# A decoder step with product-key experts: the gate table written by scattering DMAs instead of one-hot products, the sample tokens' experts gathered in the trunk

## The chip, the cores and the metric

One core of a Trainium2 chip runs the whole program in one launch. The metric is the device time of an execution in microseconds. The core has TensorE (PE, matmuls; PEld are its weight loads), VectorE (DVE), ScalarE (ACT), GpSimd (POOL, which also issues indirect DMAs) and SyncE (SP, which issues the plain DMAs).

## The reference, cut to what matters

1024 prompt tokens and 64 sample tokens (8 sequences of 8) go through one decoder layer with the same weights, in float32, width 1024:

```
xn = rmsnorm(x);  lru_x, lru_gate, q, k, v, ga, gb = split(xn @ w_in)
A = rglru(conv(lru_x)) * gelu(lru_gate);  B = window_attention(q, k, v)
hres = x + (sigmoid(ga) * (A @ w_branch_lru) + sigmoid(gb) * (B @ w_branch_attn)) @ w_out
xt = rmsnorm(hres);  qr = xt @ w_query                  # 8 heads x 2 x 128
s_top, i_top = top_k(qr . sub_keys, 16)                 # of 128, per head and half
best, pos = top_k(s_top[0] + s_top[1], 16)              # of 256 sums, per head
idx = i_top[0] * 128 + i_top[1] at pos;  g = softmax(best)   # 128 experts of 16384 per token
y = hres + sum_e gelu(xt . U[idx_e]) * g_e * V[idx_e]
```

So each token needs 128 rows of U and 128 rows of V, of 1024 numbers each.

## The kernel before, in words

**Precision.** A float32 matrix is split into a part hi, rounded to the matmul's format, and lo = x - hi. `split` does hi on ACT (line 148) and lo on VectorE or GpSimd (line 149); `mm3` multiplies hi x hi, hi x lo and lo x hi (lines 168 to 170), three matmuls for each tile of weights.

**Trunk.** `trunk` runs three times, over blocks of 256 prompt tokens with the 64 sample tokens (320 columns), 384 and 384 prompt tokens. Each block goes through attention, the gates with `w_branch_attn`, the recurrent branch (`lru`), the merge with `w_branch_lru`, `w_out`, the second norm, and `retrieve` (the product with `w_query`, the sub-keys and the sixteen best of each half). Weights come through SP's queue in pieces of 512 KB (`load_c`, `load_n`), three raw buffers and three split ones, 84 pieces for each block; GpSimd computes their lo parts.

**Which experts.** `choose` takes a block's tokens in tiles of 128 rows and finds for each head the sixteen best of 50 candidate sums and, by comparing positions (`eq`, VectorE, with a product on GpSimd), the experts' numbers.

**Two ways to apply experts.** The last block's 384 tokens (NA) are *gathered*: for each of 3 tiles and 128 slots GpSimd issues an indirect DMA that fetches one row of U (later of V) for each of the 128 tokens, and VectorE multiplies and sums it (lines 847 and 859). The other 704 tokens (ND, sample tokens among them) are *dense*: `dense` multiplies them with all 16384 rows of U and V, 128 experts e at a time, in two halves of 352 columns, and weights the activations with a table `g_d` of gates, which is zero where a token doesn't use an expert. Gathers run beside the dense loop: after each e some are issued (`pump`), so that all are done after 120 (PACE) of the 128.

**The gate table before.** For every 4 dense tokens `build_g` makes one-hot matrices of the upper and lower half of the experts' numbers (lines 889 and 890), multiplies the first with the gates in three bf16 parts (891 on GpSimd, 892, 893) and lets 12 matmuls add them into a 128x128 table per token (896 to 898); ACT copies it out (899), and SP writes 2 MB for 32 tokens (901). `slots_T` has transposed indices and gates before that.

**Order.** The functions `choose` and `build_g` of one block are generators. The next block's trunk takes a number of their steps (`bg`, numbers in PG1 and PG2) after chosen instructions, and all that is left at its end. The framework's planner then orders instructions on each engine by priority and simulated time, and each engine runs its list in order. The last block's `choose` runs at the start of the dense stage, before the gathers.

Of the kernel before, what the change touches and what calls it, by code (L numbers as in the profile page):

```python
# [8 lines left out]
F32 = mybir.dt.float32  # L9
# [10 lines left out]
P = 128  # L20
# [34 lines left out]
PAUSE = 17  # L55
# [7 lines left out]
CH = 32  # L63
# [6 lines left out]
class Kern:  # L70
    def __init__(self, ctx, tc, i, o):
# [8 lines left out]
        self.g_d = self.dr.tile([ND // CH, P, P, CH], F32, name="g_d")  # L80
        self.kcar_d = self.dr.tile([P, NKV, P], F32, name="kcar_d")
        self.sT_d = self.dr.tile([P, 3, ND], F32, name="sT_d")
        self.xn2h_d = self.dr.tile([P, KD, ND], F32, name="xn2h_d")
        self.xn2l_d = self.dr.tile([P, KD, ND], F32, name="xn2l_d")
        self.xn2n_d = self.dr.tile([NA, D], F32, name="xn2n_d")

    def setup(self, c):
# [5 lines left out]
        nc.vector.tensor_copy(self.iota, iota[:, 0:NCAND])  # L93
        self.iota4 = c.tile([P, P, 4], BF16, name="iota4")
        nc.vector.tensor_copy(self.iota4, iota.unsqueeze(2).to_broadcast([P, P, 4]))
# [90 lines left out]
    def load_c(self, src, c0):  # L186

        nc, sp = self.nc, self.sp
        hi = sp.tile([P, KD, P], F32R, tag="whi", name="whi", bufs=NW)
        lo = sp.tile([P, KD, P], F32R, tag="wlo", name="wlo", bufs=NW)  # L190
        raw = sp.tile([P, KD, P], F32, tag="wraw", name="wraw", bufs=NR)
        nc.sync.dma_start(raw, src.rearrange("(k p) c -> p k c", p=P)[:, :, c0:c0 + P])
        self.split(hi, lo, raw, nc.gpsimd)
        return hi, lo

    def load_n(self, src, c0):
# [3 lines left out]
        for h in range(2):  # L200
# [4 lines left out]
            self.split(hi, lo, raw, nc.gpsimd)  # L205
# [61 lines left out]
    def trunk(self, bi, x, raw, bg):  # L267
# [5 lines left out]
        self.pg = PG2 if bi == len(BLOCKS) - 1 else PG1  # L273
# [4 lines left out]
        self.attention(bi, xh, xl, ah, al, raw, bg)  # L278

# [17 lines left out]
        self.otag = "s4"  # L297
        self.lru(bi, n, nP, xh, xl, lh, ll, bg)
        self.otag = "sb"
# [36 lines left out]
        for t, (c0, r) in enumerate(tiles):  # L336
            keep = self.xn2n_d[r0 + c0 - ND:r0 + c0 - ND + r, :] if r0 >= ND else None
            self.norm_T(hr[0:r, t, :], r, gb, yh, yl, c0, keep)
            bg(self.pg[4])
        if r0 < ND:  # L340
            nc.sync.dma_start(self.xn2h_d[:, :, r0:r0 + n], f32(yh))
            nc.sync.dma_start(self.xn2l_d[:, :, r0:r0 + n], f32(yl))
# [24 lines left out]
    def attention(self, bi, xh, xl, ah, al, raw, bg):  # L367
# [46 lines left out]
        def scores(t, j, qT):  # L414
# [28 lines left out]
            nc.gpsimd.tensor_tensor(sb[:, :, 0:S], sb[:, :, 0:S], z4.unsqueeze(2).to_broadcast([P, 4, S]), op=ALU.mult)  # L443
# [299 lines left out]
    def choose(self, bi):  # L743
# [5 lines left out]
        late = []  # L749
        for t, (c0, r) in enumerate(tiles):  # L750
# [21 lines left out]
            for h in range(PH):  # L772
# [7 lines left out]
                yield  # L780
            bf = xp.tile([P, PH, TOPK], F32, tag="bf", name="bf", bufs=1)
            nc.vector.tensor_copy(bf[0:r], bi_[0:r])
            ev = xp.tile([P, PH, TOPK], F32, tag="ev", name="ev", bufs=1)
            for h in range(PH):
                eq = xp.tile([P, TOPK, NCAND], F32, tag="eq", name="eq", bufs=2)
                nc.vector.tensor_tensor(eq[0:r], self.iota[0:r].unsqueeze(1).to_broadcast([r, TOPK, NCAND]),
                                        bf[0:r, h].unsqueeze(2).to_broadcast([r, TOPK, NCAND]), op=ALU.is_equal)
                nc.gpsimd.tensor_tensor(eq[0:r], eq[0:r], ce[0:r, h].unsqueeze(1).to_broadcast([r, TOPK, NCAND]), op=ALU.mult)
                nc.vector.tensor_reduce(ev[0:r, h], eq[0:r], axis=AX.X, op=ALU.add)
                yield  # L790

            if r0 >= ND:
                gv = self.gA[:, t]
            else:
                ft = xp.tile([P, 3, NSLOT], F32, tag="ft", name="ft", bufs=2)
                gv = ft[:, 2].rearrange("p (h s) -> p h s", h=PH)
# [6 lines left out]
            nc.vector.tensor_tensor(gv[0:r], bv[0:r], sz[0:r].unsqueeze(2).to_broadcast([r, PH, TOPK]), op=ALU.mult)  # L803
            if r0 >= ND:
                nc.vector.tensor_copy(self.iA[:, t], ev)
            else:
                e32 = xp.tile([P, NSLOT], I32, tag="bi", name="e32", bufs=1)
                i12 = xp.tile([P, 2, NSLOT], I32, tag="cd", name="i12", bufs=1)
                nc.vector.tensor_copy(e32[0:r], ev[0:r].rearrange("p h s -> p (h s)"))
                nc.vector.tensor_scalar(i12[0:r, 0], e32[0:r], 7, None, op0=ALU.arith_shift_right)  # L810
                nc.vector.tensor_scalar(i12[0:r, 1], e32[0:r], 127, None, op0=ALU.bitwise_and)
                nc.vector.tensor_copy(ft[0:r, 0:2], i12[0:r])
                late.append((ft, r, r0 + c0))
                if len(late) > 1:
                    self.slots_T(*late.pop(0))
                yield
        for u in late:
            for _ in range(PAUSE):
                yield
            self.slots_T(*u)  # L820

    def slots_T(self, ft, r, n0):

        nc = self.nc
        pt = self.tr((P, 3, P))
        for x in range(3):
            nc.tensor.transpose(pt[:, x, 0:r], ft[0:r, x], self.ident[0:r, 0:r])
        sl = self.xp.tile([P, 3, P], F32, tag="sl", name="sl", bufs=1)
        nc.scalar.copy(sl[:, :, 0:r], pt[:, :, 0:r])
        nc.sync.dma_start(self.sT_d[:, :, n0:n0 + r], sl[:, :, 0:r])  # L830


    def gather_steps(self, gp, gps):
        nc, i, o = self.nc, self.i, self.o
        for t in range(NA // P):
# [16 lines left out]
            nc.sync.dma_start(st, self.hres_d[ND + t * P:ND + (t + 1) * P, :])  # L852
# [10 lines left out]
            nc.sync.dma_start(o["y"][ND + t * P:ND + (t + 1) * P, :], st)  # L863
# [6 lines left out]
    def build_g(self, bi):  # L870

        nc, sp = self.nc, self.sp
        p0, p1, smp, nP, n, tiles = self.geom(bi)
        for ch in range(ROW0[bi] // CH, (ROW0[bi] + n) // CH):
            sg = sp.tile([P, AT], F32, tag="at", name="sg", bufs=1)[:, 0:P * CH].rearrange("p (i n) -> p i n", i=P)
            sT = sp.tile([P, 3, CH], F32, tag="sT", name="sT", bufs=1)
            nc.sync.dma_start(sT, self.sT_d[:, :, ch * CH:(ch + 1) * CH])

            s16 = sp.tile([P, 5, CH], BF16, tag="s16", name="s16", bufs=1)
            nc.scalar.copy(s16[:, 0:3], sT)  # L880
            for x in (2, 3):
                nc.vector.tensor_tensor(sT[:, 2], sT[:, 2], s16[:, x], op=ALU.subtract)
                nc.vector.tensor_copy(s16[:, x + 1], sT[:, 2])
            for t4 in range(CH // 4):
                n0 = t4 * 4
                col = lambda x: s16[:, x, n0:n0 + 4].unsqueeze(1).to_broadcast([P, P, 4])
                oij = self.sp.tile([P, 4, P, 4], BF16, tag=self.otag, name="oij", bufs=N4 if self.otag == "s4" else 6)
                oj, wh, wm, wl = (oij[:, x] for x in range(4))
                nc.vector.tensor_tensor(oj, self.iota4, col(1), op=ALU.is_equal)
                nc.vector.tensor_tensor(wh, self.iota4, col(0), op=ALU.is_equal)  # L890
                nc.gpsimd.tensor_tensor(wl, wh, col(4), op=ALU.mult)  # L891
                nc.vector.tensor_tensor(wm, wh, col(3), op=ALU.mult)
# [208 lines left out]
```

## Time and profile before

| | us |
|---|---|
| median of 3 runs (lowest, highest) | 4002.96 (3999.92, 4014.38) |
| the profiled execution | 3999.96 |
| its span, first to last instruction | 3998.0 |
| PE, DVE, ACT, POOL busy | 3641.4 (91%), 3151.0 (79%), 1290.8 (32%), 2407.2 (60%) |
| DMA | 821.75 MB, 206 GB/s over the span |

Busy times are shares of the span over stages with different limits. Matmuls are pipelined, and the trace models their ends, so that the busy times of neighbouring ones overlap; how fast a stream of them runs is seen from start to start. The granted clock is a share of TensorE's full speed. An idle time is put down to the instruction that ended it.

### The profile page before, as it was taken

Reading aid. Unit: us, or ns where it says so; the run is one execution under the profiler, and the core shown is the slowest. Engines: PE = TensorE matmul, PEld = TensorE weight load, DVE = VectorE, ACT = ScalarE, POOL = GpSimd, SP = SyncE. Lnnn points to the kernel's source line nnn. Section 1 sums busy time; section 2 is a strip of 40 time slices with the busy share of each in tenths; the row PEclk is TensorE's granted clock in tenths of the full one; section 3 lists DMA queues with packets and bytes.
Section 4 is the critical chain, followed back from the end, with each engine's and each line's share of the span. In section 5 each row is a group of like instructions: output and inputs, shape, how many; then the busy total and the mean of one; then the engine's idle time right before and its main releaser. Section 6 shows DMA issues by size and latency. Waiting matters only on the chain. (4 is left out here: it accounts for less than half of the span.)

```text
span 3998.0 us, 60600 instructions
## 1 busy us (share of the span) xinstructions
PE 3641.4 (91%) x22734; PEld 3477.6 (87%) x22734; DVE 3151.0 (79%) x6798; ACT 1290.8 (32%) x2346; POOL 2407.2 (60%) x1560
## 2 busy tenths in 40 slices
PE   7988998778897878998899999999999999999998
PEld 6778978668895777888799999999999999999998
DVE  6365787999899988998987777777777777777773
ACT  4454353443333435333222222222222222222221
POOL 3444546565554664764576677767766767676651
PEclk8989999889997988999899999999999999999999
DMA  5334523234441133444359898999989899899972
GB/s 148 100 111 149 154 72 90 79 101 145 171 139 56 58 94 108 138 173 162 125 204 308 292 318 303 321 323 316 322 295 311 306 319 316 309 317 310 319 259 80
DMA packets 505654, 821.75 MB, mean 206 GB/s; under 512 B 34220, under 2 KB 360812, under 8 KB 502000
## 3 DMA queue, kind: packets, MB, share of 16 engines
q1 hardware_dynamic: 394768, 415.18, 32.5%
q0 software_dynamic: 110592, 402.70, 28.2%
q8 instruction: 178, 2.92, 0.3%
q14 instruction: 116, 0.95, 0.1%
HBM read 753.25 MB, written 66.50 MB: 205 GB/s over the span
## 5 line engine op out<-in xcount | busy, mean ns | idle before, releaser
L149 POOL TENSOR_TENSOR wlo<-wraw,whi 128x1024 fp32r<-128x1024 f32 x252 | 639.3, 2544 | 513.7 <-ACT whi L148 476.0
L168 PE MATMUL ou<-ah,vh 128*128 128x352 f32 x2048 | 663.4, 327 | 40.6 <-ACT ah L148 23.3
L168 PE MATMUL sc<-dx,uh 128*128 128x352 f32 x2048 | 664.6, 325 | 16.2 <-ACT uh L148 9.0
L169 PE MATMUL ou<-al,vh 128*128 128x352 f32 x2048 | 660.1, 325 | 5.3 <-DVE al L149 5.0
L170 PE MATMUL sc<-dx,ul 128*128 128x352 f32 x2048 | 662.0, 323 | 1.0 <-POOL ul L149 1.0
L169 PE MATMUL sc<-dx,uh 128*128 128x352 f32 x2048 | 662.5, 324 | 0.0
L170 PE MATMUL ou<-ah,vl 128*128 128x352 f32 x2048 | 659.0, 324 | 0.0
L859 DVE SCALAR_TENSOR_TENSOR acc<-row,hv,acc 128x1024 f32<-128x1024 f32 x384 | 493.1, 1284 | 157.3 <-DMA row<-in_expert_v,iA 151.6
L847 DVE SCALAR_TENSOR_TENSOR row<-row,xt 128x1024 f32<-128x1024 f32 x384 | 465.5, 1217 | 174.3 <-DMA row<-in_expert_u,iA 165.0
L857 POOL DMA_INDIRECT row<-in_expert_v,iA x384 | 362.2, 943 | 267.8 <-DVE acc L859 192.6
L845 POOL DMA_INDIRECT row<-in_expert_u,iA x384 | 362.4, 944 | 264.4 <-DVE row L847 187.4
L168 PEld LDWEIGHTS ou<-ah,vh 128*128 128x128 f32 x2048 | 385.0, 189 | 55.7 <-ACT ah L148 29.7
L168 PEld LDWEIGHTS sc<-dx,uh 128*128 128x128 f32 x2048 | 386.9, 189 | 20.0 <-DVE al L149 9.8
L148 ACT CAST whi<-wraw 128x1024 fp32r<-128x1024 f32 x252 | 263.9, 1049 | 429.6 <-PE mm L169 167.6
L169 PEld LDWEIGHTS ou<-al,vh 128*128 128x128 f32 x2048 | 387.0, 189 | 7.8 <-DVE al L149 7.8
L170 PEld LDWEIGHTS sc<-dx,ul 128*128 128x128 f32 x2048 | 386.5, 189 | 1.4 <-POOL ul L149 1.4
L169 PEld LDWEIGHTS sc<-dx,uh 128*128 128x128 f32 x2048 | 387.2, 189 | 0.0
L170 PEld LDWEIGHTS ou<-ah,vl 128*128 128x128 f32 x2048 | 386.8, 189 | 0.0
L970 DVE TENSOR_TENSOR dac<-dac,ou 128x352 f32<-128x352 f32 x672 | 339.3, 514 | 59.9 <-PE ou L170 58.0
L149 POOL TENSOR_TENSOR vl<-vn,vh 128x1024 fp32r<-128x1024 f32 x128 | 309.0, 2422 | 65.6 <-ACT vh L148 38.5
L149 POOL TENSOR_TENSOR ul<-un,uh 128x1024 fp32r<-128x1024 f32 x128 | 310.7, 2427 | 45.7 <-ACT uh L148 43.6
L891 POOL TENSOR_TENSOR oij<-oij,s 128x512 bf16<-128x512 bf16 x176 | 225.1, 1290 | 176.9 <-DVE oij L890 132.7
(287 smaller groups left out, 8484.5 us busy)
## 6 DMA issues: line engine op xcount, KB each, us to landing
wraw<-in_w_in SPq DMA_DIRECT2D x132, 512.0 KB
un<-in_expert_uT SPq DMA_DIRECT2D x128, 512.0 KB
vn<-in_expert_v SPq DMA_DIRECT2D x128, 512.0 KB
g_d<-sg SPq DMA_DIRECT2D x22, 2048.0 KB
gt<-g_d SPq DMA_DIRECT2D x64, 704.0 KB
wraw<-in_peer_w_query SPq DMA_DIRECT2D x48, 512.0 KB
wraw<-in_w_branch_attn SPq DMA_DIRECT2D x24, 512.0 KB
wraw<-in_w_branch_lru SPq DMA_DIRECT2D x24, 512.0 KB
```

What stands on the lines that cost most here:

```text
L148: nc.scalar.copy(hi, src)
L149: return (lo_eng or nc.vector).tensor_tensor(lo, src, f32(hi), op=ALU.subtract)
L168: nc.tensor.matmul(ps, lh, rh, start=first and j == 0, stop=False)
L169: nc.tensor.matmul(ps, lh, rl, start=False, stop=False)
L170: nc.tensor.matmul(ps, ll, rh, start=False, stop=last and j == n - 1)
L845: nc.gpsimd.indirect_dma_start(out=row, out_offset=None, in_=i["expert_u"], in_offset=bass.IndirectOffsetOnAxis(ap=ia[:, s:s + 1], axis=0))
L847: nc.vector.scalar_tensor_tensor(row, row, 1.0, xt, op0=ALU.mult, op1=ALU.mult, accum_out=hv[:, s:s + 1])
L857: nc.gpsimd.indirect_dma_start(out=row, out_offset=None, in_=i["expert_v"], in_offset=bass.IndirectOffsetOnAxis(ap=ia[:, s:s + 1], axis=0))
L859: nc.vector.scalar_tensor_tensor(acc, row, hv[:, s:s + 1], acc, op0=ALU.mult, op1=ALU.add)
L891: nc.gpsimd.tensor_tensor(wl, wh, col(4), op=ALU.mult)
L970: nc.vector.tensor_tensor(ac[k // 4][:, k % 4, a:b], ac[k // 4][:, k % 4, a:b], ps[:, 0:b - a], op=ALU.add)
```

## The change

The dense stage takes 640 tokens, all prompt tokens of the first two blocks, in two parts of 256 and 384 columns (before: 704, in 352 and 352). The gate table is ten tables of 64 tokens. `zero_g` zeroes them in the first block with 40 DMAs of 1 MB from a zero tile. `choose` computes for each slot the position expert x 64 + token in its table, and `chain` issues 64 indirect DMAs for each table, which add one weight each for 128 (token, slot) pairs: 640 scatters in all. Scatters into the same table follow one another; those of different tables take turns. `slots_T` and `build_g` go.

The 64 sample tokens' experts are gathered in the trunk, two slots in one DMA (64 tokens on each half of the partitions): 64 rows of U in the second block (`early_u`), 64 of V in the third (`early_v`). `behind` mixes a step of `choose`, one of the early gathers and three (second block) or four (third) scatters into each background step.

The lo parts of all trunk weights, and the scaling of the attention's probabilities, go from GpSimd to VectorE. The expert's number is found by subtracting positions and taking the smallest absolute value, without GpSimd.

```diff
-ND = NTOT - NA
+ND = NTOT - NA - NS
+COL0 = [0, BLOCKS[0][1]]
+RA = ROW0[-1]
+NT2 = 64
+STEP = 32768
+SCAT = (3, 4)
-PAUSE = 17
+PG0 = (1, 1, 1, 0, 0, 0, 0, 0)
...
-        self.g_d = self.dr.tile([ND // CH, P, P, CH], F32, name="g_d")
+        self.g_d = [self.dr.tile([P * P * NT2, 1], F32, name="g%d" % t) for t in range(ND // NT2)]
...
 (load_c and load_n)
-        self.split(hi, lo, raw, nc.gpsimd)
+        self.split(hi, lo, raw)
...
-            nc.gpsimd.tensor_tensor(sb[:, :, 0:S], sb[:, :, 0:S], z4.unsqueeze(2).to_broadcast([P, 4, S]), op=ALU.mult)
+            nc.vector.tensor_tensor(sb[:, :, 0:S], sb[:, :, 0:S], z4.unsqueeze(2).to_broadcast([P, 4, S]), op=ALU.mult)
...
 (choose)
+            nc.vector.tensor_tensor(ce[0:r], ce[0:r], self.iota[0:r].unsqueeze(1).to_broadcast([r, PH, NCAND]), op=ALU.add)
             for h in range(PH):
-                eq = xp.tile([P, TOPK, NCAND], F32, tag="eq", name="eq", bufs=2)
-                nc.vector.tensor_tensor(eq[0:r], self.iota[0:r].unsqueeze(1).to_broadcast([r, TOPK, NCAND]),
-                                        bf[0:r, h].unsqueeze(2).to_broadcast([r, TOPK, NCAND]), op=ALU.is_equal)
-                nc.gpsimd.tensor_tensor(eq[0:r], eq[0:r], ce[0:r, h].unsqueeze(1).to_broadcast([r, TOPK, NCAND]), op=ALU.mult)
-                nc.vector.tensor_reduce(ev[0:r, h], eq[0:r], axis=AX.X, op=ALU.add)
+                eq = xp.tile([P, TOPK, NCAND], F32, tag="eq", name="eq", bufs=1)
+                nc.vector.tensor_tensor(eq[0:r], ce[0:r, h].unsqueeze(1).to_broadcast([r, TOPK, NCAND]),
+                                        bf[0:r, h].unsqueeze(2).to_broadcast([r, TOPK, NCAND]), op=ALU.subtract)
+                nc.vector.tensor_reduce(ev[0:r, h], eq[0:r], axis=AX.X, op=ALU.min, apply_absolute_value=True)
...
+                for hf in range(2):
+                    for a in range(2):
+                        nc.sync.dma_start(fx[a * NT2:(a + 1) * NT2, hf], ft[hf * NT2:(hf + 1) * NT2, a])
+                    chains.append(self.chain(self.g_d[(COL0[bi] + c0) // NT2 + hf], fx, hf))
...
+    def zero_g(self):
+        for g in self.g_d:
+            for m in range(4):
+                dst = g.rearrange("(j x y) o -> j x (y o)", j=P, y=512)[:, 4 * m:4 * m + 4, :]
+                nc.sync.dma_start(dst, self.zero.unsqueeze(1).to_broadcast([P, 4, 512]))
+                yield
+
+    def chain(self, tab, fx, hf):
+        for s in range(NSLOT // 2):
+            self.nc.gpsimd.indirect_dma_start(out=tab, out_offset=bass.IndirectOffsetOnAxis(ap=fx[:, hf, 0, s:s + 1].bitcast(I32), axis=0),
+                                              in_=fx[:, hf, 1, s:s + 1], in_offset=None, compute_op=ALU.add)
+            yield True
+
+    def early_u(self):
...
+        for s in range(NSLOT // 2):
+            row = et[:, D * (1 + s % 3):D * (2 + s % 3)]
+            nc.gpsimd.indirect_dma_start(out=row, out_offset=None, in_=self.i["expert_u"],
+                                         in_offset=bass.IndirectOffsetOnAxis(ap=self.es[:, 0, s:s + 1].bitcast(I32), axis=0))
+            nc.vector.scalar_tensor_tensor(row, row, 1.0, xt, op0=ALU.mult, op1=ALU.mult, accum_out=self.eh[:, s:s + 1])
+            yield True
...
+    def behind(self, b):
+        chains, early = [], None
+        ch = self.choose(b, chains)
+        left = True
+        while left or chains or early is not False:
+            if b == 0 and early is None and self.es is not None and self.at_free:
+                early = self.early_u()
+            if b == 1 and early is None and self.at_free:
+                early = self.early_v()
+            if left:
+                left = next(ch, None) is not None
+            if early and next(early, None) is None:
+                early = False
+            for _ in range(SCAT[b]):
+                if chains:
+                    c = chains.pop(0)
+                    if next(c, None) is not None:
+                        chains.append(c)
+            yield True
...
 (dense)
-        H = ND // 2
-        halves = [(0, H), (H, ND)]
+        halves = [(0, COL0[1]), (COL0[1], ND)]
...
-                            gts.append(up.tile([P, H // CH, 4, CH], F32, tag="gt", name="gt", bufs=3))
-                            nc.sync.dma_start(gts[-1], self.g_d[a // CH:b // CH, :, e:e + 4, :].rearrange("c j e n -> j c e n"))
+                            gts.append(up.tile([P, 6, 4, NT2], F32, tag="gt", name="gt", bufs=3)[:, 0:(b - a) // NT2])
+                            for x in range(a // NT2, b // NT2):
+                                src = self.g_d[x].rearrange("(j i n) o -> j i (n o)", j=P, i=P)
+                                nc.sync.dma_start(gts[-1][:, x - a // NT2], src[:, e:e + 4, :])
...
 (run)
-            steps = iter(())
+            steps = self.zero_g()
...
-                steps = itertools.chain(self.choose(b), self.build_g(b))
+                steps = self.behind(b)
```

## Rows read from the trace of the kernel before

**Rows 1.** Table of stretches: window, length, busy us (instructions), granted clock, DMA share, GB/s.

```profile
core 0: us, PE busy (x) PEld busy (x) DVE busy (x) ACT busy (x) POOL busy (x), PEclk, DMA share, GB/s
0.00:521.00 521.00, 450.93 (x3053) 416.06 (x3053) 318.47 (x1037) 244.09 (x502) 235.63 (x103) 0.92 0.44 132
521.00:1920.00 1399.00, 1178.66 (x7349) 1073.51 (x7348) 1258.07 (x3132) 557.20 (x1055) 783.88 (x410) 0.91 0.35 113
1920.00:3998.00 2078.00, 2011.76 (x12336) 1988.04 (x12335) 1574.48 (x2630) 489.54 (x789) 1387.70 (x1048) 0.99 0.83 286
2048.00:3850.00 1802.00, 1760.00 (x10831) 1742.95 (x10830) 1385.12 (x2197) 425.26 (x691) 1258.45 (x983) 1.00 0.90 312
```

**Rows 2.** Waits, total us, times, longest: three of 2100 to 3800, one of 521 to 1920.

```profile
ACT uh L148 <- PE sc L169: 288.6, 41, 14.9
POOL row L845 <- DVE row L847: 179.6, 163, 8.8
DVE row L847 <- DMA row<-in_expert_u,iA: 152.5, 124, 5.0
...
PE tr L896 <- DVE oij L893: 52.1, 26, 6.1
```

**Rows 3.** Groups of VectorE by line and shape, whole span.

```profile
L893 DVE TENSOR_TENSOR oij<-oij,s 128x512 bf16<-128x512 bf16 x176 | 156.0, 902 | 7.2 <-POOL oij L891 7.1
L892 DVE TENSOR_TENSOR oij<-oij,s 128x512 bf16<-128x512 bf16 x176 | 127.7, 743 | 0.2
L889 DVE TENSOR_TENSOR oij<-iota,s 128x512 bf16<-128x512 bf16 x176 | 114.6, 651 | 27.1 <-PE tr L898 27.0
L890 DVE TENSOR_TENSOR oij<-iota,s 128x512 bf16<-128x512 bf16 x176 | 100.2, 569 | 0.0
...
L882 DVE TENSOR_TENSOR sT<-sT,s 128x32 f32<-128x32 f32 x44 | 23.6, 537 | 9.2 <-ACT s L880 8.9
```

**Rows 4.** Single lines: count, shortest/median/longest ns, first and last start us.

```profile
L661 DVE TENSOR_TENSOR U<-U,Y x8: 940/1368/4165, 754.4 to 1604.7; 128x768 f32<-128x768 f32 x8
L308 DVE TENSOR_TENSOR mg<-mg,th x24: 476/546/2609, 334.5 to 1727.2; 128x384 f32<-128x384 f32 x16, 128x320 f32<-128x320 f32 x8
L149 POOL TENSOR_TENSOR wlo<-wraw,whi x252: 2332/2403/6124, 15.9 to 1893.0; 128x1024 fp32r<-128x1024 f32 x126
```

**Rows 5.** The same view: prices of a subtraction and a comparison, and the softmax scaling.

```profile
L149 DVE TENSOR_TENSOR ll<-ge,lh x16: 542/548/2714, 770.1 to 1616.7; 128x384 fp32r<-128x384 f32 x16
L786 DVE TENSOR_TENSOR eq<-iota,bf x72: 964/990/3216, 650.9 to 2038.3; 128x800 f32<-128x800 f32 x64, 64x800 f32<-64x800 f32 x8
L443 POOL TENSOR_TENSOR sb<-sb,sm x32: 1040/1894/2714, 98.3 to 1335.8; 128x1024 f32<-128x1024 f32 x28, 128x512 f32<-128x512 f32 x4
```

**Rows 6.** TensorE in order of time (start, duration): first and last of three unbroken runs.

```profile
2024.74 0.32 PE L169 MATMUL ou<-al,vh 128*128 128x352 f32 x1
...
2031.29 0.33 PE L169 MATMUL sc<-dx,uh 128*128 128x352 f32 x1
...
916.00 0.34 PE L168 MATMUL mm<-lh,whi 128*128 128x384 f32 x1
...
920.85 0.34 PE L169 MATMUL mm<-xl,whi 128*128 128x384 f32 x1
...
1786.18 0.28 PE L169 MATMUL mm<-wlo,gh 128*128 128x256 f32 x1
...
1788.91 0.28 PE L169 MATMUL mm<-wlo,gh 128*128 128x256 f32 x1
```

**Rows 7.** A gather and its uses: lines, then two issues in order of time.

```profile
L845 POOL DMA_INDIRECT row<-in_expert_u,iA x384: 935/941/1108, 2044.2 to 3565.3; - x192
L847 DVE SCALAR_TENSOR_TENSOR row<-row,xt x384: 1207/1216/1224, 2051.8 to 3570.7; 128x1024 f32<-128x1024 f32 x192
L859 DVE SCALAR_TENSOR_TENSOR acc<-row,hv,acc x384: 1275/1283/1292, 2358.4 to 3875.0; 128x1024 f32<-128x1024 f32 x192
...
3014.32 0.95 POOL L857 DMA_INDIRECT row<-in_expert_v,iA  x1 [0.16 <-issue]
3015.57 0.94 POOL L857 DMA_INDIRECT row<-in_expert_v,iA  x1 [0.30 <-issue]
```

**Rows 8.** Table of stretches: one slice of 10 us.

```profile
2640.00:2650.00 10.00, 9.18 (x58) 9.17 (x58) 7.07 (x11) 2.31 (x4) 8.03 (x6) 1.00 1.06 383
```

More of the change, by code (lines that the diff above doesn't have):

```diff
@@ L748, in choose @@
         r0 = ROW0[bi]
-        late = []
-        for t, (c0, r) in enumerate(tiles):
+        for t, (c0, r) in sorted(enumerate(tiles), key=lambda x: x[1][1]):
             fi = xp.tile([P, 16, TOPK], F32, tag="fi", name="fi", bufs=1)
@@ L817, in choose @@
[L817 to L830, printed above, removed]
+                continue
@@ L867, in pump @@
             next(self.steps, None)
[L870 to L892, printed above, removed]
-                nc.vector.tensor_tensor(wh, wh, col(2), op=ALU.mult)
-                pt = self.tr()
-                for x in range(4):
-                    nc.tensor.matmul(pt[:, x, :], oj[:, :, x], wh[:, :, x], start=True, stop=False)
-                    nc.tensor.matmul(pt[:, x, :], oj[:, :, x], wm[:, :, x], start=False, stop=False)
-                    nc.tensor.matmul(pt[:, x, :], oj[:, :, x], wl[:, :, x], start=False, stop=True)
-                nc.scalar.copy(sg[:, :, t4 * 4:t4 * 4 + 4], pt.rearrange("p x i -> p i x"))
-                if t4 == CH // 4 - 1:
-                    nc.sync.dma_start(self.g_d[ch], sg)
-                yield
@@ new lines, in early_u @@
+    def early_u(self):
+        nc = self.nc
+        et = self.sp.tile([P, AT], F32, tag="at", name="et", bufs=1)
+        xt = et[:, 0:D]
+        for a in range(2):
+            nc.sync.dma_start(et[a * NS:(a + 1) * NS, 0:D], self.xn2n_d[NA:, :])
+        for s in range(NSLOT // 2):
[3 more added lines that the diff above has]
+            nc.vector.scalar_tensor_tensor(row, row, 1.0, xt, op0=ALU.mult, op1=ALU.mult, accum_out=self.eh[:, s:s + 1])
+            yield True
+        nc.scalar.activation(self.eh, self.eh, AF.Gelu_apprx_tanh)
+        nc.vector.tensor_tensor(self.eh, self.eh, self.es[:, 1], op=ALU.mult)
+        yield True
@@ new lines, in early_v @@
+    def early_v(self):
+        nc = self.nc
+        et = self.sp.tile([P, AT], F32, tag="at", name="et", bufs=1)
+        acc = et[:, 0:D]
+        row = lambda s: et[:, D * (1 + s % 3):D * (2 + s % 3)]
+        for s in range(NSLOT // 2):
+            nc.gpsimd.indirect_dma_start(out=row(s), out_offset=None, in_=self.i["expert_v"],
+                                         in_offset=bass.IndirectOffsetOnAxis(ap=self.es[:, 0, s:s + 1].bitcast(I32), axis=0))
+            if s == 0:
+                nc.vector.tensor_scalar(acc, row(s), self.eh[:, 0:1], None, op0=ALU.mult)
+            else:
+                nc.vector.scalar_tensor_tensor(acc, row(s), self.eh[:, s:s + 1], acc, op0=ALU.mult, op1=ALU.add)
+            yield True
+        r0 = BLOCKS[0][1]
+        nc.sync.dma_start(row(0)[0:NS], acc[NS:P])
+        nc.sync.dma_start(row(1)[0:NS], self.hres_d[r0:r0 + NS, :])
+        nc.vector.tensor_tensor(acc[0:NS], acc[0:NS], row(0)[0:NS], op=ALU.add)
+        nc.vector.tensor_tensor(acc[0:NS], acc[0:NS], row(1)[0:NS], op=ALU.add)
+        nc.sync.dma_start(self.o["y"][r0:r0 + NS, :], acc[0:NS])
+        yield True
```

95 lines of the change are left out of this document (56 added, 39 removed).

## The prediction, written before the changed kernel was run

> **What bounds the kernel now.** I read the table of stretches first, then the waits, then the groups by line. The profiled execution took 3999.96 us, 2 us above its span of 3998.0; the median of the runs shown is 4002.96, so a sum made against 4000 stands 3 us under it. The table [rows 1] cuts the span into the first block (0 to 521 us, nothing in the background), the other two blocks (521 to 1920) and the dense stage from 1920 on. In the dense stage TensorE is busy 97% at the full clock (0.99), and the DMA engines 90% once the gathers run (2048 to 3850): two resources near full, TensorE a little ahead. The waits of that stage [rows 2] agree: ACT waits for TensorE to give weight buffers back (288.6 us), while GpSimd waits 179.6 us for VectorE to free a row buffer and VectorE 152.5 us for rows to land, so the gather loop has little slack. In blocks two and three VectorE is busy 1258 of 1399 us, 90% [rows 1], TensorE 84% at clock 0.91, and the longest wait of TensorE is for VectorE's one-hot products (52.1 us, [rows 2]). I take VectorE as the bound there.
>
> **The change part by part.**
>
> Dense matmuls. Before, each of 6144 pairs of matmuls has 352 and 352 columns; afterwards 256 and 384. From start to start, 41 steps of the 352 form take 6.55 us (0.160 us), 28 of the 384 form 4.85 us (0.173), 24 of the 256 form 2.73 us (0.114) [rows 6]. A pair goes from 0.320 to 0.287 us: 6144 x 0.0325 = 200 us less, if TensorE stays the bound. What is late next is the DMA. The gather stretch, 1802 us at 312 GB/s, moves 562 MB [rows 1]; the table slices lose one eleventh of their bytes, about 4 MB. Shrunk by 0.287/0.320 the stretch would be 1619 us: 558 MB at 345 GB/s, and the busy share scales to 0.90 x 1802/1619 x 558/562 = 0.99. Single slices of 10 us reach 383 GB/s [rows 8], so 345 isn't a wall, but the queue is full and landings come later. Bounds: all 200, or only the 10% of the 240 us with matmuls but no gathers (24 us). I take 160, nearer the upper end because of the slices.
>
> The removed one-hot build. In blocks two and three VectorE loses 176 times four products: 156.0 + 127.7 + 114.6 + 100.2 us, and 23.6 us of the split of the weights in three parts [rows 3]: 522 us. TensorE loses 2112 small matmuls, ACT 176 copies; neither is the bound, so I count nothing for them.
>
> The lo halves move from GpSimd to VectorE. Of 252 [rows 4], 84 lie in each block. The same kind of subtraction is 548 ns for 384 elements, a two-input comparison 990 for 800 [rows 5]; the line through both gives 1.23 us for 1024. Blocks two and three: 168 x 1.23 = 207 us more. The softmax scaling moves too: 24 of the 32 [rows 5] lie there, 24 x 1.2 = 29 us. GpSimd is freed of all elementwise work in the trunk.
>
> What that takes off VectorE besides. Its instructions are stretched beside GpSimd's: a 128x768 product has 940 ns at its shortest and 4165 at its longest, a 128x384 sum 546 in the median and 2609 at most, and the excess is the size of one GpSimd subtraction (2403 ns median) [rows 4]. Busy time less count times median, over some two dozen kept lines of the two blocks, leaves about 150 us (an estimate; bounds 0, if the new DMA issues hold VectorE as well, and 200). I take 150. By the Trainium skill ("SBUF — State Buffer", Who interferes with whom) a VectorE instruction with two SBUF inputs and a GpSimd one that reads SBUF lock each other out for the whole instruction, which the stretched rows bear out; without this rule's lock the 150 us would be 0 and the sum below 3770.
>
> The sample tokens' gathers. 64 rows of U and 64 of V: on VectorE 64 x (1.22 + 0.08) and 64 x 1.28 us, the dense stage's prices [rows 7], 165 us in blocks two and three; the choice of experts gains an addition and an index calculation per tile, about 10. On GpSimd a gather takes 1.25 us from start to start [rows 7].
>
> VectorE in the two blocks: 1258 - 522 - 150 + 207 + 29 + 165 + 10 = 997 us. At the same 90% that is 1108 us against 1399, 291 less. TensorE's own work, and norms and attention where the engines take turns, will not shrink alike; I count two thirds, 190 us. Bounds: 291, and below nothing by the rivals on GpSimd.
>
> The scatters. 640 of them (256 in block two over four tables, 384 in block three over six), each of 128 single weights, each waiting on GpSimd for the one before on its table. The trace has no scatter and no adding DMA. The nearest row is the gather, 1.25 us per issue: 768 x 1.25 = 960 of 1399 us, which hides. The other end is a landing of some 10 us waited for in full: with four and six tables in rotation 2.5 and 1.7 us each, 640 + 640 us plus 160 of gathers, 1440 in all, just more than the stretch. I take the gather's price. By the Trainium skill ("SBUF — State Buffer", SBUF: two separate sides) GpSimd can't write DMA descriptors while VectorE runs a two-port copy or scalar operation. The rows show one long issue among 384 (1108 against a median of 941 ns, [rows 7]), but beside a VectorE that runs other kinds; if half of the 768 issues met 0.5 us of such work the queue would hold 190 us more, still inside the stretch.
>
> The first block. VectorE gets 84 x 1.23 + 8 x 1.2 = 113 us more in a block where it had 203 us idle [rows 1]; little of it is behind TensorE's two spare weight buffers, most of it falls where TensorE is ahead. The 40 zeroing DMAs of 1 MB go onto SP's queue in front of weights. 22 go out one by one; 18 are left at the block's end, in front of the second block's weights: 18.9 MB at 312 GB/s would be 60 us if nothing hid them. The block's DMA share is 0.44 [rows 1], and part of block two's weights is loaded ahead. Together I take 25 us more, between 0 and 170.
>
> Sum: 4000 + 25 - 190 - 160 = 3675; I forecast 3675 us.
>
> **The rivals.**
>
> A. VectorE waits in order for the sample rows, which stand on GpSimd behind three or four scatters each, and behind VectorE's wait stand the lo halves that TensorE needs. For it: 64 early steps of block three at five issues each are 64 x 5 x 1.25 = 400 us, and they stand in the middle of a block that lasts some 700 (half of the 1399). Against it: the planner may put other VectorE work ahead. The two blocks then gain nothing: 4000 + 25 - 160 = 3865.
>
> B. The dense stage is held by the gathers. For it: a DMA share of 0.99 needed, and the waits on row buffers already there [rows 2]. Against it: the slices at 383 GB/s. Dense gains 24: 4000 + 25 - 190 - 24 = 3811.
>
> C. The other side: the scatter chains on GpSimd. An adding scatter reads, adds and writes; if it costs s on GpSimd or in waiting, 640 s + 160 us must fit into 1399 plus what the dense stage gains: it decides from s = (1399 + 135 - 160)/640 = 2.1 us. At 2.5 us the two blocks take 1760: 4000 + 25 + 361 - 160 = 4226. For it: no row excludes it. Against it: at most a quarter to a sixth of a landing shows in each, and a landing would have to be over 10 us.
>
> **How the numbers follow.** The forecast 0.50 (its own range 3530 to 3790), A 0.20, B 0.13, C 0.12, and 0.05 that A and B come together near 4000. What a measurement of this kernel can tell from no change is about 0.5%, 20 us. Faster: 0.50 + 0.20 + 0.13 = 0.83; the last 0.05 is split over same (0.04) and slower (0.01), which with C makes 0.13. The range 3530 to 3920 holds the forecast, A and B less their edges, some 0.8.
>
> **What would show it.** In the table of stretches the dense stage should begin near 1755 and last some 1915 us with a DMA share over 0.93; VectorE in the two blocks near 1000 busy us, no trunk line of it with a 2.5 us maximum. If scatters are cheap, their start to start is near 1.25 us and GpSimd's queue ends before the dense stage; if A holds, VectorE's idle time before the early rows is over 100 us; if C, GpSimd's wait for its own scatters is the longest of all and the first table slice of the dense stage waits for them. The prediction is wrong if the trunk doesn't shrink although VectorE's busy time does.

## The result, and the profile after

The changed kernel takes 4200.76 us (median of 4 runs, 4196.3 to 4205.35) against 4003.59 us of the kernel before beside it: ratio 1.0488, 95% interval 1.0464 to 1.0512. It is slower by 197 us where I forecast 325 us faster, and outside my range of 3530 to 3920. The profiled execution took 4196.3 us, its span is 4194.5.

First the page of the changed kernel: busy tenths of TensorE and GpSimd in 40 slices of 105 us, the granted clock, and the DMA share.

```profile
PE   3598999769982055567400899999999999999998
POOL 0000000367788888888888677777767777677774
PEclk7689999879986577788755999999999999999999
DMA  9634632777632255577322889889988998989887
```

TensorE has three holes: at the start, around slice 13, and in slices 19 to 21. Through the last two GpSimd stands at 8 tenths. The table of stretches of the same kernel gives their size (columns as in [rows 1]; the first block ends near 586 us here, 65 us later than before by its first product with `yh`, 506.3 against 441.7 us):

```profile
0.00:100.00 100.00, 41.87 (x260) 38.21 (x260) 35.11 (x153) 23.13 (x44) 0.20 (x4) 0.77 0.98 355
...
586.00:2314.00 1728.00, 963.06 (x5186) 866.29 (x5185) 1021.06 (x3076) 456.07 (x851) 1225.21 (x768) 0.76 0.48 104
1300.00:1400.00 100.00, 0.00 (x0) 0.00 (x0) 0.00 (x0) 0.00 (x0) 83.56 (x55) 0.50 0.22 0
2100.00:2200.00 100.00, 0.00 (x0) 0.00 (x0) 23.10 (x56) 1.33 (x2) 83.86 (x54) 0.50 0.25 11
2314.00:4194.00 1880.00, 1830.64 (x12328) 1815.58 (x12328) 1434.17 (x2365) 466.95 (x780) 1339.32 (x1024) 0.99 0.89 313
```

Blocks two and three take 1728 us instead of 1399 [rows 1], though VectorE, which I took as their bound, is busy only 1021 us in them: it no longer sets the time. The dense stage takes 1880 instead of 2078. So 65 + 329 - 198 = 196 us: the loss is in the two blocks, and 65 us of it in the first. The lines of the instructions concerned (count, shortest/median/longest ns, first and last start us):

```profile
L895 SPq DMA_DIRECT2D g<-zero x40: 360/2628/5358, 16.9 to 125.0; - x40
...
L901 POOL DMA_INDIRECT g<-fx x640: 1542/1546/3377, 887.4 to 2305.8; - x160
...
L162 DVE TENSOR_TENSOR wlo<-wraw,whi x252: 1165/1217/1299, 17.9 to 2019.6; 128x1024 fp32r<-128x1024 f32 x126
...
L321 DVE TENSOR_TENSOR mg<-mg,th x24: 483/546/566, 410.5 to 1874.0; 128x384 f32<-128x384 f32 x16, 128x320 f32<-128x320 f32 x8
```

A scatter holds GpSimd 1.546 us at the median and 1.675 in the mean, with 0.29 us of issue between two; the first starts at 887 us, the last at 2306. The waits of the whole execution (total us, times, longest), of the stops of TensorE and VectorE alone:

```profile
PE sc L181 <- DMA gt<-g: 273.8, 1, 273.8
...
PE mm L181 <- DVE fi L771: 208.0, 1, 208.0
...
DVE et L932 <- DMA et<-in_expert_v,est: 207.8, 1, 207.8
```

The first score product of the dense stage waits 273.8 us for its table slice. The stop of 208 us is VectorE's, for its first gathered row of V, with TensorE behind it. In order of time, the end of that stop:

```profile
1480.48 1.55 POOL L901 DMA_INDIRECT g<-fx  x1 [0.30 <-issue]
1482.33 1.55 POOL L901 DMA_INDIRECT g<-fx  x1 [0.30 <-issue]
1484.18 1.00 POOL L929 DMA_INDIRECT et<-in_expert_v,est  x1 [0.30 <-issue]
...
1488.51 0.75 DVE L932 TENSOR_SCALAR et<-et,eh 128x1024 f32<-128x1024 f32 x1 [207.81 <-DMA et<-in_expert_v,est]
```

Scatter follows scatter at 1.85 us. The gather of the row that VectorE wants stood behind all those issued before it on GpSimd, and VectorE, which works in order, stood with it.

### The profile page after: what moved, and what is told of

Read it like the earlier page. It is cut to its first block, busy times and chain, and to the rows that moved or that the text cites. A ratio compares the mean times of both kernels' runs of the same rounds, so it can differ in the third digit from the quotient of the medians.

```text
span 4194.5 us, 56211 instructions
## 1 busy us (share of the span) xinstructions
PE 3255.1 (78%) x20596; PEld 3111.5 (74%) x20596; DVE 2793.4 (67%) x6494; ACT 1171.0 (28%) x2138; POOL 2564.7 (61%) x1796
## 5 line engine op out<-in xcount | busy, mean ns | idle before, releaser
L901 POOL DMA_INDIRECT g<-fx x640 | 1071.9, 1675 | 224.5 <-issue 185.6
L181 PE MATMUL sc<-dx,uh 128*128 128x256 f32 (+1 forms) x2048 | 634.0, 310 | 273.9 <-DMA gt<-g 273.8
L181 PE MATMUL ou<-ah,vh 128*128 128x384 f32 (+1 forms) x2048 | 629.9, 312 | 36.5 <-ACT ah L161 27.8
L183 PE MATMUL sc<-dx,ul 128*128 128x256 f32 (+1 forms) x2048 | 632.6, 309 | 1.0 <-POOL ul L162 1.0
L182 PE MATMUL sc<-dx,uh 128*128 128x256 f32 (+1 forms) x2048 | 633.3, 309 | 0.0
L182 PE MATMUL ou<-al,vh 128*128 128x384 f32 (+1 forms) x2048 | 629.3, 310 | 0.5 <-DVE al L162 0.3
L183 PE MATMUL ou<-ah,vl 128*128 128x384 f32 (+1 forms) x2048 | 628.4, 309 | 0.0
L914 POOL DMA_INDIRECT et<-in_expert_u,est x64 | 77.6, 1212 | 837.7 <-DVE c L793 758.2
L181 PE MATMUL mm<-xh,whi 128*128 128x384 f32 (+1 forms) x768 | 271.7, 354 | 263.7 <-DVE fi L771 208.0
L162 DVE TENSOR_TENSOR wlo<-wraw,whi 128x1024 fp32r<-128x1024 f32 x252 | 306.5, 1217 | 154.2 <-ACT whi L161 153.7
L181 PEld LDWEIGHTS mm<-xh,whi 128*128 128x128 f32 x768 | 157.6, 205 | 276.7 <-issue 230.3
```

The costliest lines, as they stand in the source:

```text
L162: return (lo_eng or nc.vector).tensor_tensor(lo, src, f32(hi), op=ALU.subtract)
L181: nc.tensor.matmul(ps, lh, rh, start=first and j == 0, stop=False)
L182: nc.tensor.matmul(ps, lh, rl, start=False, stop=False)
L183: nc.tensor.matmul(ps, ll, rh, start=False, stop=last and j == n - 1)
L901: self.nc.gpsimd.indirect_dma_start(out=tab, out_offset=bass.IndirectOffsetOnAxis(ap=fx[:, hf, 0, s:s + 1].bitcast(I32), axis=0), in_=fx[: ...
L914: nc.gpsimd.indirect_dma_start(out=row, out_offset=None, in_=self.i["expert_u"], in_offset=bass.IndirectOffsetOnAxis(ap=self.es[:, 0, s:s ...
```

## The experiments

Theory Q: the queue of 640 scatters on GpSimd sets the end. Rival Z: the zero writes at the start; rival O: VectorE's wait in order for the sample rows (A of the prediction); R: something else in the later blocks. The times of all runs, and from each trace where the scatters stand (us); ratios are against the kernel before on the same chip.

| run | time | ratio (95% interval) | first, last scatter | first score product |
|---|---|---|---|---|
| changed kernel | 4200.76 | 1.0488 (1.0464 to 1.0512) | 887.4, 2305.8 | 2314.1 |
| e1_paced_zero | 4135.9 | 1.0353 (1.0323 to 1.0384) | 823.5, 2238.9 | 2246.9 |
| e2_early_unread | 4102.98 | 1.0271 (1.0241 to 1.0301) | 831.0, 2226.7 | 2234.7 |
| e3_half_scatters | 3804.94 | 0.9525 (0.9497 to 0.9553) | 877.6, 1749.8 | 1820.5 |
| e4_plain_scatter | 4182.13 | 1.0469 (1.0399 to 1.054) | 877.8, 2099.5 | 2316.8 |
| e5_no_scatters | 3618.85 | 0.9048 (0.9025 to 0.9071) | none | 1635.9 |
| e6_half_rows | 4137.08 | 1.033 (1.0308 to 1.0352) | 888.3, 2229.5 | 2237.1 |
| o1_onehot640 | 3876.68 | 0.97 (0.9676 to 0.9724) | none | 1894.5 |
| o2_onehot640_pool | 4019.22 | 1.0051 (1.0035 to 1.0067) | none | 2028.4 |
| h1_mixed | 3953.98 | 0.9899 (0.9868 to 0.9931) | 802.0, 1365.4 | 1964.9 |
| h2_mixed_own | 3943.74 | 0.9842 (0.9826 to 0.9859) | 789.6, 1357.2 | 1947.6 |
| o3_rows5 | 3771.13 | 0.9407 (0.9391 to 0.9423) | none | 1899.2 |
| h3_mixed_rows5 | 3821.0 | 0.9533 (0.951 to 0.9557) | 804.7, 1367.5 | 1959.4 |

**The zero writes (e1).** Each zero write waits for a small clear on VectorE, so that they spread over the first block:

```diff
-PG0 = (1, 1, 1, 0, 0, 0, 0, 0)
+PG0 = (1, 1, 1, 1, 1, 1, 0, 0)
...
-                dst = g.rearrange("(j x y) o -> j x (y o)", j=P, y=512)[:, 4 * m:4 * m + 4, :]
-                nc.sync.dma_start(dst, self.zero.unsqueeze(1).to_broadcast([P, 4, 512]))
+                z = self.xp.tile([P, 2 * NSLOT], F32, tag="fx", name="z", bufs=4)
+                nc.vector.memset(z, 0.0)
+                dst = g.rearrange("(j x y) o -> j x (y o)", j=P, y=256)[:, 8 * m:8 * m + 8, :]
+                nc.sync.dma_start(dst, z.unsqueeze(1).to_broadcast([P, 8, 256]))
```

> The tables are zeroed at the pace of the first block: each 1 MB write waits for a small memset on VectorE that stands behind the block's own work, instead of all 40 going out in the first 125 us. Theory Q (GpSimd's queue bounds the trunk: the scatters run without a gap from 887 us on, and the dense stage waits for the last): TensorE's 50 us stop behind the zeroing and the slow start of the first block go, the queue starts some 85 us earlier and so does everything behind it: 4200 - 85 = 4115 us. Rival Z (the zeroing costs nothing that counts, since the queue is late for another reason): 4200 us, with the first block still ending near 600 us.

4135.9, near Q's 4115: 65 us of the loss. The writes now start between 176.9 and 442.6 us, the first product with `yh` comes at 432.2 instead of 506.3, the first scatter 64 us earlier, the last one 67. The zeroing cost what it delayed the start of the queue; it isn't the cause.

**VectorE's order (e2).** The early rows are gathered but VectorE doesn't read them (the sample tokens' sums are left out).

```diff
-            nc.vector.scalar_tensor_tensor(row, row, 1.0, xt, op0=ALU.mult, op1=ALU.mult, accum_out=self.eh[:, s:s + 1])
...
-                nc.vector.tensor_scalar(acc, row(s), self.eh[:, 0:1], None, op0=ALU.mult)
-            else:
-                nc.vector.scalar_tensor_tensor(acc, row(s), self.eh[:, s:s + 1], acc, op0=ALU.mult, op1=ALU.add)
+                nc.vector.memset(acc, 0.0)
```

> The sample tokens' rows are still gathered, but VectorE doesn't read them (the sample tokens' expert sums are left out), so that VectorE never waits for a gather in the trunk. Theory Q: the 208 us stop of VectorE and TensorE near 1280 us goes, the trunk ends earlier, but the last scatter doesn't; TensorE waits for the first table slice over 400 us instead of 274, and the time stays at 4200 (4170 to 4210). Rival O (what costs is the order: VectorE stands in line for a row behind scatters): the 208 us come off, 3990 us.

4102.98, under Q's 4170 to 4210 and over O's 3990: neither time came. The lines say why. First TensorE's longest waits in the later blocks, then a wait of SP's queue, then the scatters:

```profile
PE sc L181 <- DMA gt<-g: 372.4, 1, 372.4
PE mm L181 <- ACT gh L328: 211.3, 1, 211.3
```

```profile
SPq L936 <- DMA et<-in_expert_v,est: 219.9, 1, 219.9
```

```profile
L901 POOL DMA_INDIRECT g<-fx x640: 1543/1545/3517, 831.0 to 2226.7; - x160
```

VectorE's stop of 208 us is gone, but the trunk still stands, 211.3 us: at line 936 SP, whose queue works in order, waits 219.9 us for the V rows, which stand behind the scatters, and the weights of `w_out` stand behind SP's wait. So the edit moved O's stop and didn't remove it. Yet the dense stage's wait for its table grows by 99 us, from 273.8 to 372.4, and the stage still begins 8 us after the last scatter. The queue begins 56 us earlier and is 22 us shorter (1396 instead of 1418), and the dense stage begins 79 us earlier: most of the 98 us gained. The earlier start comes from the U rows: in the changed kernel 34 of their 64 products stand on VectorE before the step of the choice that the first scatter needs (line 837), which comes at 866.5 us there and at 811.4 here. O's stop of the trunk is real, but covered by the queue.

**Half the scatters (e3) and none (e5).** Each table gets 32 scatters instead of 64 (half the gate weights are left out), or none (`chain` returns at once).

```diff
-        for s in range(NSLOT // 2):
+        for s in range(NSLOT // 4):
```

> Only 32 of the 64 scatters of each table are issued (half of the gate weights are left out). Theory Q: 320 x 1.95 = 624 us come off GpSimd's queue, more than it is late by; the trunk is then bound by its own work, the dense stage starts near 1900 to 1980 us and the time is 3780 to 3860. Rival O: the planner's order still makes VectorE wait for the rows, but behind half as many scatters; some 100 of the 208 us and half of the wait at the end come off: about 3960.

> The changed kernel with all 640 scatters left out (the gate tables stay zero; the zero writes, the choice of experts, the early sample rows and the 640-token dense part stay). Theory Q (the whole loss is the scatter queue on GpSimd): nothing holds the trunk or the first table slice any more, the dense part begins at 1700 to 1770 us and the kernel takes 3600 to 3700 us, which is near what I forecast for the change. Rival R (the two later blocks are held by something else as well, the early rows or VectorE's added lo halves): the dense part does not begin before about 1820 us, where it began with half the scatters, and the time is 3750 us or more.

3804.94 and 3618.85: Q's times both, R is out; the dense stage begins even earlier than I had put it for Q (1820.5 and 1635.9). The scatters, with all that waits behind them, cost 4201 - 3619 = 582 us, and without them the kernel lands 56 us below my forecast. Its table of stretches:

```profile
581.00:1636.00 1055.00, 908.76 (x5195) 825.10 (x5193) 943.82 (x2805) 454.98 (x847) 181.05 (x129) 0.92 0.55 169
1636.00:3620.00 1984.00, 1844.94 (x12328) 1827.05 (x12328) 1525.43 (x2638) 476.05 (x789) 1341.71 (x1024) 0.97 0.85 297
```

With half of them the queue ends at 1750, 71 us before the dense stage: no longer the bound. The stage still begins 185 us later than with none, and the waits of its later blocks show VectorE held by the V rows behind scatters (the same wait without scatters, in e5, is 14.3 us):

```profile
DVE et L934 <- DMA et<-in_expert_v,est: 166.5, 55, 10.4
```

**What in a scatter costs: the addition (e4), the words (e6).**

```diff
-                                              in_=fx[:, hf, 1, s:s + 1], in_offset=None, compute_op=ALU.add)
+                                              in_=fx[:, hf, 1, s:s + 1], in_offset=None)
```

```diff
-            self.nc.gpsimd.indirect_dma_start(out=tab, out_offset=bass.IndirectOffsetOnAxis(ap=fx[:, hf, 0, s:s + 1].bitcast(I32), axis=0),
-                                              in_=fx[:, hf, 1, s:s + 1], in_offset=None, compute_op=ALU.add)
+            self.nc.gpsimd.indirect_dma_start(out=tab, out_offset=bass.IndirectOffsetOnAxis(ap=fx[0:64, hf, 0, s:s + 1].bitcast(I32), axis=0),
+                                              in_=fx[0:64, hf, 1, s:s + 1], in_offset=None, compute_op=ALU.add)
```

> The 640 scatters write their weights instead of adding them (an expert that two heads of a token choose keeps one weight). If it is the adding that makes a scatter take 1.55 us of GpSimd and not 0.94 like a gather, each falls to about 0.95 + 0.30 from start to start, the queue holds 640 x 0.6 = 384 us less, and the time is near 3820. If the price is that of any scatter of single numbers, the row stays at 1.55 us and the time at 4200.

> All 640 scatters stay, but each adds only the words of the first 64 partitions (half of the gate weights are left out). If a scatter's price goes by its words, one takes about 0.8 to 1.1 us of GpSimd instead of 1.55 and the kernel comes near the run with half the scatters, 3780 to 3870 us. If it goes by the instruction, 1.55 us stays and so does the time, 4150 to 4200 us.

The scatters' lines, e4 and then e6:

```profile
L901 POOL DMA_INDIRECT g<-fx x640: 955/962/2568, 877.8 to 2099.5; - x160
```

```profile
L901 POOL DMA_INDIRECT g<-fx x640: 1402/1411/4702, 888.3 to 2229.5; - x160
```

Half the words save 0.135 us of 1.546: nearly all of the price goes by the instruction, as the second theory had it. The queue is 77 us shorter, the kernel 64 us faster, 13 us under that theory's times. The addition is 0.58 of the 1.546 us; without it a scatter has the gather's price (0.96 against 0.941, [rows 7]). By e4's time alone I would have said that the addition costs nothing, and that would have been wrong: its queue ends 206 us earlier, and the dense stage begins at the same time. The hundred microseconds after 1100 and 1900 in e4 show TensorE at 14%, and VectorE and the DMA engines nearly idle as well:

```profile
1100.00:1200.00 100.00, 14.22 (x35) 9.45 (x36) 6.36 (x32) 1.52 (x2) 75.93 (x80) 0.50 0.04 6
1900.00:2000.00 100.00, 13.41 (x36) 10.24 (x36) 3.26 (x4) 1.04 (x1) 76.25 (x79) 0.50 0.05 9
```

and its waits have some that the changed kernel has not, first of all engines, then of TensorE from 880 to 2330 us:

```profile
ACT whi L161 <- remote: 343.8, 12, 129.2
...
DVE hr L339 <- remote: 223.8, 5, 98.4
```

```profile
PE mm L181 <- issue: 124.2, 61, 4.9
```

ACT and VectorE wait there for events whose sender the trace doesn't name ("remote"), and TensorE's matmuls start one by one, two or more us apart, with nothing in the trace that holds them ("issue"; in the changed kernel TensorE waits 0.8 us like this in the same stretch). The trunk slows while plain scatters pass at 1.27 us from start to start, and the saving is spent. Why, no run here settles.

The Trainium skill ("DMA: Bandwidth & Descriptors", Anatomy of one DMA — SWDGE (gpsimd) path) calls the part of a DMA's fixed cost that grows with descriptors small, so that many can be emitted before it shows. e6 agrees: 64 words fewer save 0.135 us of 1.546.

**The table without scatters (o1, o2).** The 640-token dense part and the early rows stay; the table is built by the one-hot compares and products of the kernel before (`slots_T`, `build_g`, for 640 tokens), without zero writes. In o2 the lo halves go back to GpSimd:

```diff
-        self.split(hi, lo, raw)
+        self.split(hi, lo, raw, nc.gpsimd)
```

> The change without its scatters: the table is built by the one-hot compares and products of the kernel before, for 640 tokens, with no zero writes; early sample rows, lo halves on VectorE and the 640-token dense part stay. By VectorE's sum (997 us busy in the changed kernel's two later blocks plus 160 groups at 2.87 us = 459, and about 140 us not busy) the dense part begins near 2120 us and, at 1850 to 1880 us of dense part, the kernel takes 3950 to 4000 us: no gain over before. Rival (the one-hot groups fall into waits of VectorE that are there anyway): the dense part begins near 1920 us as before, 3770 to 3820 us.

> As the run with the one-hot table for 640 tokens, but the lo halves of the weights on GpSimd as in the kernel before. VectorE is spared 207 us of subtractions and gets about 150 us of stretched instructions back: 40 to 60 us faster than that run, 3900 to 3950 us. Rival (in a kernel without scatters GpSimd is free, so taking 172 subtractions off VectorE gives the whole 207 us): 3760 to 3800 us. Second rival (the stretch costs more than the subtractions): slower than that run.

3876.68 and 4019.22. o1 beats both kernels; its time is 73 us under my range and 57 over the rival's. o2 falls to its second rival, the stretch. The table of stretches for blocks two and three, and the last one-hot product of a group, first of o1, then of o2:

```profile
493.00:1894.00 1401.00, 1160.61 (x7122) 1054.04 (x7120) 1273.71 (x3513) 552.69 (x1032) 375.75 (x288) 0.88 0.49 158
```

```profile
L926 DVE TENSOR_TENSOR oij<-oij,s 128x512 bf16<-128x512 bf16 x160 | 98.2, 629 | 8.0 <-POOL oij L924 7.9
```

```profile
521.00:2028.00 1507.00, 1190.99 (x7149) 1075.74 (x7147) 1377.51 (x3269) 552.16 (x1038) 755.83 (x449) 0.87 0.46 147
```

```profile
L926 DVE TENSOR_TENSOR oij<-oij,s 128x512 bf16<-128x512 bf16 x160 | 137.6, 878 | 14.0 <-POOL oij L924 13.8
```

In o1's stretch VectorE does 160 subtractions that GpSimd does in o2 (201 us) and is still busy 104 us less. So the neighbour on GpSimd stretched VectorE's other work by some 300 us in o2 (an estimate from these two numbers); I had put the stretch at 150. Four products of a one-hot group take 2.13 us in o1, 2.65 in o2 and 2.83 before [rows 3]. I had priced o1's groups by the stretched rows: 160 x (2.87 - 2.13) = 118 us, about half of what the dense part begins before my 2120. The Trainium skill ("SBUF — State Buffer", Who interferes with whom) has this as an exclusive lock on a port pair that VectorE and GpSimd share; that some 200 us of added work on VectorE in these blocks make the kernel 142 us faster bears the rule out.

**Part scatter, part one-hot (h1, h2).** The first block's 256 tokens are scattered, the second's 384 go by one-hot. h1 let the second block's slots share a buffer with the scatters' inputs; h2 gives them their own, and transposes them tile by tile:

```diff
-                ft3 = xp.tile([P, 3, NSLOT], F32, tag="fx", name="ft3", bufs=2)
+                ft3 = xp.tile([P, 3, NSLOT], F32, tag="ft3", name="ft3", bufs=1)
...
-                if len(late) > 1:
-                    self.slots_T(*late.pop(0))
+                self.slots_T(*late.pop(0))
```

> The first block's 256 tokens by scatters (256 of them, zero writes of their 4 tables paced), the second block's 384 tokens by the one-hot compares; the rest as in the change. Theory Q: 256 scatters at 1.95 us are 500 us of GpSimd, which fit beside the second block (from about 880 to 1380 us), and the third block takes 96 one-hot groups of 2.87 us, 275 us of VectorE: the dense part begins at 1850 to 1960 us, the time is 3720 to 3830 us, faster than both kernels. Rival (each scatter costs the kernel the same wherever it stands: 396 us gained by leaving out 320 is 1.24 us each): 4201 - 384 x 1.24 + 275 = 4000 us.

> The mixed table again (256 tokens scattered, 384 by one-hot), with a buffer of its own for the second block's slots, which in the first try shared one with the scatters' inputs: VectorE waited 138.9 us there for the scatters to end, and stood before attention's rows. If that hold was the miss, it goes whole: 3780 to 3830 us. If the scatters held the second block in another way too (each costing 1.24 us of the kernel wherever it stands), it stays at 3900 us or more.

3953.98 and 3943.74, slower than o1. Both miss my forecast; h1 is 46 us under its rival's time, and h2 lies where its rival had it (3900 or more). The longest waits of VectorE in them, h1 and then h2:

```profile
DVE ft L843 <- DMA g<-fx: 138.9, 1, 138.9
```

```profile
DVE oij L963 <- POOL oij L961: 170.8, 8, 163.3
```

The stop only moved. In h2 VectorE waits 163.3 us for a one-hot product of GpSimd, which stood behind the scatters until the last one at 1357.2; the product itself took 1.63 us, at 1358.3. Both are O's mechanism with another victim: one long stop, and not a price on each scatter as the rival had it. How much of the time each stop costs is not shown; a version in which nothing that VectorE needs stands behind the scatters was not tried.

**The gathered rows (o3, h3).** o1 and h2 with five buffers for the dense stage's rows, of U and of V:

```diff
-                row = gp.tile([P, D], F32, tag="row", name="row", bufs=4)
+                row = gp.tile([P, D], F32, tag="row", name="row", bufs=5)
```

> The one-hot table for 640 tokens with five buffers instead of four for the gathered rows of the dense part. In the run with four the last row is used at about 3860 us and TensorE's last score product is at 3758: 768 rows take 1850 us in four runs alike. If the four buffers set that (issue, landing and use of a row over four), the rows end with the products: 3790 to 3830 us. If the DMA engines set it (share 0.89 in the dense part), 3860 to 3880 us, no change.

> The mixed table with its own slot buffer and with five row buffers: what each of the two gives by the two runs beside it, added: 3700 to 3760 us if both theories hold, 3780 to 3830 if only the slot buffer's does.

3771.13 and 3821.0: 105 and 123 us, more than I expected. (h3's time lies where I had put it for the slot buffer alone, by chance: there the slot buffer gained little and the row buffers much.) o3 is the fastest kernel here that leaves nothing out, 5.9% below the one before. The last use of a row and the middle of the dense stage, o1 and then o3:

```profile
L892 DVE SCALAR_TENSOR_TENSOR acc<-row,hv,acc x384: 1276/1284/1292, 2335.9 to 3862.3; 128x1024 f32<-128x1024 f32 x192
```

```profile
2650.00:3150.00 500.00, 488.83 (x3289) 485.49 (x3288) 383.21 (x656) 126.41 (x210) 358.87 (x275) 0.99 0.90 312
```

```profile
L892 DVE SCALAR_TENSOR_TENSOR acc<-row,hv,acc x384: 1274/1281/1292, 2316.2 to 3768.9; 128x1024 f32<-128x1024 f32 x192
```

```profile
2650.00:3150.00 500.00, 497.21 (x3389) 495.84 (x3388) 403.80 (x669) 128.60 (x215) 381.79 (x294) 1.00 0.93 330
```

From the first gather to the last use the 768 rows take 1748 us instead of 1846. In the 500 us shown the DMA share rises from 0.90 to 0.93 and the rate from 312 to 330 GB/s: four buffers were the limit, not the DMA engines.

## Why the prediction was wrong

- **The failed step: the scatters**, "768 x 1.25 = 960 of 1399 us, which hides". Both numbers failed. A scatter costs GpSimd 1.675 us and 0.29 of issue, 1.96 in all (640 x 1.96 = 1257 of the queue's 1418 us), not a gather's 1.25. And the queue cannot use 1399 us: its first entry needs the first block's choice of experts, and stands at 887 us, not at 521 (without the zero writes' delay at 823.5, e1; without the U rows' products at 831.0, e2). The table shows the bound: in the changed kernel, e1, e2 and e6 the first score product comes 8 us after the last scatter starts. The prediction's other end for GpSimd, 1440 us, came near the queue's 1418 by luck: it priced each scatter by a landing of some 10 us, which no run shows (the last scatter's landing and the load of the first table slice take those 8 us together).
- **Rival C** named the place, but its rule ("it decides from s = 2.1 us") used the same 1399 us and so would have passed the measured 1.96; that its 4226 us lie near the 4201 is luck too, since they were worked out with 2.5 us for each scatter. From 887 us to the dense begin that I forecast, 1755, there are 868 us: even the gathers' price, 640 x 1.25 = 800 and 64 rows of V at 1.25, 880 in all, would have filled them. That could have been read blind: before, the choice's comparisons start at 650.9 us [rows 5], and in that trace the first matmul of the one-hot table, which needs the same choice, stands at 864.5, 890 us before 1755. Nor was GpSimd's "wait for its own scatters" the sign that I named (35.9 us in 30 times): the time is in the instructions themselves.
- **Rival A** happened, 207.8 us of VectorE idle before the first V row, over the 100 that I named; e2 shows that the queue covers it, and e3, h1 and h2 that it, or a like stop, holds VectorE where the queue does not.
- **VectorE in blocks two and three**: forecast 997 us busy. The changed kernel's 1021 are no match for it: they hold the third block's choice (72 comparisons in the stretch against 48), whose last step there comes at 2123.8 us, inside the wait for the table. Without scatters (e5), with that choice in the dense stage as before, it is 944. So the prediction's own sign of being wrong came true in the changed kernel: VectorE's busy time shrank and the trunk didn't. In e5 the stretch of 1055 us is 344 less than before, not the 190 that I counted, with VectorE busy 89% of it, about the 90% that I had assumed: the discount to two thirds was wrong, TensorE's own share (909 us, 86%) shrank along. The subtraction's price, 1.23 us, measured 1.217; no line of the trunk is stretched (`mg`, 566 ns at most against 2609, [rows 4]).
- **The first block**: forecast 25 us more, measured 65. The 40 zero writes all stand at 16.9 to 125 us in front of weights, with a DMA share of 0.98, and none of them is left for the block's end, where I had put 18; without them (o1) the first product with `yh` is at 413.5 us, so they cost 93 us and the lo halves on VectorE gave 28, for which I had counted nothing. With the lo halves back on GpSimd (o2) it is at 440.7.
- **The dense stage**: forecast 160 us less. It is 198 less in the changed kernel, and 94 in e5. In e5 the third block's choice ends at 1753.1 us, in the dense stage, and the rows begin 118 us after the products (1754.0 and 1635.9), as before (124 us, [rows 1, 7]); in the changed kernel the choice has fallen into the wait for the table, and the rows begin 10 us after the products (2324.0 and 2314.1). So with the choice where I had it the gain was 94. Rival B was right that the gathers hold the stage, but by their buffers, not by the DMA engines: with five (o3) the stage takes 1876 us, with four (o1) 1974.

## What to carry to other kernels

An operation that the trace doesn't show is priced by measuring it or by a bound that is kept in the sum; and the stretch in which it may hide begins where its inputs are ready and ends where its result is needed, both read from the trace. A long queue on an in-order engine also holds every small thing issued behind it, so look at who waits for those before using the "free" engine. Prices taken from rows that a neighbour engine had stretched are not prices once that neighbour is gone.

## What the runs showed of the hardware

- An indirect scatter of 128 single words takes 1.546 us of GpSimd with addition, 0.962 without, 1.411 with addition of 64 words; a gather of 128 rows of 4 KB takes 0.94. Bytes hardly count in these rows, the instruction does.
- While plain scatters passed at 1.27 us from start to start, TensorE was 14% busy and the DMA engines at a share of 0.04 (e4, cause open); beside adding ones at 1.85 the trunk's `mg` line kept 566 ns at most, and the DMA share was 0.22 while TensorE stood.
- A subtraction on GpSimd of 2.4 us [rows 4] cost VectorE more than the same subtraction done by VectorE in 1.217 us: some 300 us of stretch against 201 us in two blocks, and 142 us of the kernel's time (o2 against o1).
- Five row buffers instead of four took 768 gathered rows from 1846 to 1748 us and the DMA share from 0.90 to 0.93 (o3 against o1).
